# Chunk-major mLSTM rows in DRAM, masks of the first attention head on two engines, and a first modulation made in two halves

## The chip, the cores and the metric

One core of a Trainium2 chip runs the whole layer. The metric is the device time of one execution in microseconds. PE is TensorE, DVE is VectorE, ACT is ScalarE, POOL is GpSimd and SP is SyncE; SP does no arithmetic here, its queue issues most of the DMAs.

## The reference, cut to what matters

One layer over 2048 latent tokens of 1024 features and 256 context tokens. An adaLN modulation is computed from a conditioning vector, the tokens are normalised and modulated and projected; eight heads of neighbourhood attention and four heads of a bidirectional mLSTM read the projection; an output projection and a mixture of experts follow.

```python
ada = silu(c) @ w_ada[l] + b_ada[l]             # latent tokens; ada_c from c_ctx for the context
sh1, sc1, g1, sh2, sc2, g2 = jnp.split(ada, 6, axis=-1)
z  = _modulate(_layer_norm(x), sh1, sc1) @ w_in[l]      # xn * (1 + scale) + shift
zc = _modulate(_layer_norm(ctx), csh1, csc1) @ w_in[l]
...
# neighbourhood attention, per head and grid row: window scores + relative bias, and context scores
s = concatenate([s_win + bias, s_ctx]); p = softmax(s)
...
# mLSTM: q, k = rope(silu(conv5(z)));  then per direction, per chunk of 128 tokens:
dlog = where(causal, b[:, None] - b[None, :] + i[None, :], -inf)
s    = (q_c @ k_c.T) * exp(dlog - m_t)
num  = s @ v_c + inter * (q_c @ C)
C    = decay * C + (wgt * k_c).T @ v_c
...
mix = concatenate([na, ml]) @ w_out[l];  x_mid = LN(alpha * x + g1 * mix)
out = LN(alpha * x_mid + g2 * moe(modulate(LN(x_mid), sh2, sc2)))
```

## The kernel before, in words

The kernel is written with a tile framework: tiles come from pools with a number of buffers, and a planner at compile time puts the instructions of each engine in an order, by the order of the program and by the times it reckons with. An instruction that is wrapped in `in_order` keeps its place in the program. Each engine, and the SP queue, then runs its own list strictly in order.

**Input projection (0 to about 793 us).** The tokens are worked in two halves of 1024, each in two groups of 512; the context is a third group of the first half. Products are made in three passes of split float32 (a high part and a rest of both factors): `mm_T` (L246 to L248) gives columns by tokens and `mm_N` (L255 to L257) tokens by columns; both read the modulated and transposed tokens `xhi`, `xlo` and the weights `whi`, `wlo`. `load_w` (L227) loads a weight block of 128 x 512 into one of three `wraw` buffers, casts it on ACT (L234) and makes its rest on DVE (L235). `build_group` (L159) transposes normalised tokens on PE (L170) and applies the modulation `modT` on ACT (L177, L179), with the rest on DVE (L182). `modT` comes from `first_modulation` (L185): the vectors c and c_ctx are loaded into `cc` with single elements scattered over partitions (L188, L189), passed through SiLU, and multiplied with the first 2048 columns of w_ada, 32 blocks of 128 x 512 float32 (256 KB each, loads at L207, products at L210, four column groups of PE for four blocks). One copy (L214), four transposes (L218) and two copies (L219, L220) then give all of `modT`, and only after it can `build_group` make its first piece. In the loop at L517 the first group's pieces are built pair of k by pair of k and multiplied as they come.

**mLSTM columns.** For each half and each of q and k, four heads: a product, a convolution of five taps on ACT and DVE (L631 to L638), a rotary turn with a partition shuffle through four DMAs (L645), `t1 = acc * cos` (L647, one buffer `t1`), `sw * sin` on POOL (L648), a sum (L649), and a store of 128 partitions x 1022 or 1026 float32 to `mqk_d`, laid out [partition, q or k, head, token] (L650).

**mLSTM stage (about 793 to 972 us).** 32 steps alternate between the two directions; each handles one chunk of 128 tokens for four heads. `fetch_step` (L100) runs three steps ahead into three buffers: `qk` (512 KB, runs of 128 float32 out of `mqk_d`, L104), `bcs` (256 KB, L106), `va` (256 KB, runs of 128 float32 into padded rows, L108). In a step DVE makes the exponents (four instructions of L796), the product with the scores (L816), three small operations (L836 to L838), the state's update (four of L784) and, from the 17th step on, a sum (L851); POOL makes `vw` (L802) and `qw` (L808). All of them are `in_order`. Between the steps `head(0)` (L703), a generator that is advanced once a step from step 2 on, loads the first attention head: q and k rows, nine bias tiles (i = 0 to 8), value rows; and adds a mask to each bias tile on POOL (`masked`, L719 to L721): tiles 0 to 4 from step 10 on and the others in steps 15 to 18. The masks come in three DMAs in steps 6, 10 and 14 (L862).

**Neighbourhood attention (about 972 to 1300 us).** 8 heads x 16 blocks, `scores(n)` (L940): products on PE, bias and maximum on DVE (L960, one input in PSUM and one in SBUF), exponential on ACT, transposes on PE. Head 0's blocks 0 to 3 use bias tiles 0 to 2, blocks 4 to 11 tiles 3 to 5, blocks 12 to 15 tiles 6 to 8. Then the output projection, the router and the expert loop follow in order.

The functions that the change touches:

Of the kernel before, what the change touches and what calls it, by code (L numbers as in the profile page):

```python
# [11 lines left out]
F32 = mybir.dt.float32  # L12
# [10 lines left out]
P = 128  # L23
# [12 lines left out]
def tile_layer(ctx, tc, A, out):  # L36
# [20 lines left out]
    mqk_d = dram.tile([P, 2, 4, NT], F32, name="mqk_d")  # L57
# [42 lines left out]
    def fetch_step(n):  # L100
# [3 lines left out]
        in_order(nc.sync.dma_start(qk[:], mqk_d[:, :, :, c * P : (c + 1) * P]))  # L104
# [7 lines left out]
    with ExitStack() as es, ExitStack() as zes:  # L112
# [72 lines left out]
        def first_modulation():  # L185

            cc = stp.tile([P, 2, KC], F32, name="cc", bufs=1)
            nc.sync.dma_start(cc[:, 0, :], A["c"].rearrange("o (k p) -> p (o k)", p=P))  # L188
            nc.sync.dma_start(cc[:, 1, :], A["c_ctx"].rearrange("(k p) -> p k", p=P))  # L189
            nc.gpsimd.memset(cs[:], 0.0)  # L190
            for i in range(2):
                nc.scalar.activation(cs[:, :, i], cc[:, i, :], AF.Silu)
            pa = pt.tile([P, 2, 2, P], F32, name="ptx")
            pa = pa[:].rearrange("p a b t -> p (a b t)")
            for i in range(2):
                bada = zp.tile([1, 1024], F32, name=("cosq", "sinq")[i])
                nc.sync.dma_start(bada[:], A["b_ada"][:, i * 1024 : (i + 1) * 1024])
                for j in range(2):
                    c0 = 64 * i + 32 * j
                    nc.tensor.matmul(  # L200
                        pa[c0 : c0 + 32, :], ones1[:], bada[:, j * 512 : (j + 1) * 512], start=True, stop=False, tile_position=(0, c0)
                    )
            for k in range(KC):
                wts = []
                for j in range(4):
                    wt = xg.tile([P, 512], F32, name=f"x{('hi', 'lo')[j // 2]}_{j % 2}_{k}")
                    nc.sync.dma_start(wt[:], A["w_ada"][0, k * P : (k + 1) * P, j * 512 : (j + 1) * 512])  # L207
                    wts.append(wt)
                for j in range(4):
                    nc.tensor.matmul(  # L210
                        pa[32 * j : 32 * j + 32, :], cs[:, k, :], wts[j][:], start=False, stop=k == KC - 1, tile_position=(0, 32 * j)
                    )
# [4 lines left out]
            for q in range(4):  # L217
                nc.tensor.transpose(pm[:, q, :], rows[:, q * P : (q + 1) * P], ident[:])  # L218
# [2001 lines left out]
```

## Time and profile before

| what | value |
|---|---|
| median of 3 runs (2724.01 to 2726.02) | 2725.88 us |
| the profiled execution: its own time | 2719.89 us |
| its span | 2717.9 us |
| PE busy in the span | 2481.7 us (91%) |
| DVE busy in the span | 1268.3 us (47%) |
| DMA, mean | 231 GB/s |

The span is the time from the first to the last recorded instruction; the own time of that execution is 1.99 us longer. PE's busy time says that something is in the array, not that the array is at its peak. The slices of the page divide the span into 40 parts of 67.95 us each; a digit is the busy share in tenths:

```profile
PE   8999999999997899998999679979999999999890
DVE  5547224257236976665578952222222233222226
DMA  8634762334449979994654689999689886998936
```

The first slice holds the first modulation, slices 12 to 14 (counted from 0) the mLSTM stage, the slices after that the attention.

### The profile page before, as it was taken

The numbers are of one execution on the slowest core, as the hardware profiler recorded it, in microseconds if no ns is written. First come the engines' busy times: TensorE is split into PE (matmuls) and PEld (weight loads), VectorE is DVE, ScalarE is ACT, GpSimd is POOL, SyncE is SP. The second block draws the span as 40 slices with busy tenths as digits, with TensorE's granted clock in tenths as the row PEclk, the third lists the DMA queues.
The fourth block names the chain that finished last, engine by engine and source line by source line (L and its number), as shares of the span: only waits on it lengthen the run. The fifth ranks groups of instructions, "written<-read, shape, count | busy, mean of one in ns | idle before, by whom it ended". The sixth has DMA issues, their size and how long they took to land. (4 is left out here: it accounts for less than half of the span.)

```text
span 2717.9 us, 51820 instructions
## 1 busy us (share of the span) xinstructions
PE 2481.7 (91%) x17292; PEld 1568.7 (58%) x17292; DVE 1268.3 (47%) x2882; ACT 804.9 (30%) x1707; POOL 759.1 (28%) x886
## 2 busy tenths in 40 slices
PE   8999999999997899998999679979999999999890
PEld 4778667877887778876787533323333333333330
DVE  5547224257236976665578952222222233222226
ACT  4423105243134666655565310000000000000005
POOL 1212211002034535456434422211222122221124
PEclk9999999999999999999999779989999999999995
DMA  8634762334449979994654689999689886998936
GB/s 268 178 102 134 248 219 94 140 97 158 112 137 260 265 197 214 202 212 141 183 152 151 213 308 349 366 394 340 220 281 335 312 299 223 331 328 318 381 102 263
DMA packets 286891, 626.97 MB, mean 231 GB/s; under 512 B 79448, under 2 KB 142924, under 8 KB 262444
## 3 DMA queue, kind: packets, MB, share of 16 engines
q1 hardware_dynamic: 254716, 564.87, 62.6%
q0 software_dynamic: 31696, 60.09, 9.6%
q8 instruction: 70, 1.15, 0.2%
q10 hardware_dynamic: 352, 0.39, 0.1%
q14 instruction: 57, 0.47, 0.1%
HBM read 947.01 MB, written 97.42 MB: 384 GB/s over the span
## 5 line engine op out<-in xcount | busy, mean ns | idle before, releaser
L2048 POOL DMA_INDIRECT acc_d<-y,ids x112 | 174.6, 1559 | 739.9 <-DMA acc_d<-y,ids 277.7
L2011 DVE TENSOR_TENSOR sg<-sg,ph 128x128 f32<-128x128 f32 x112 | 39.8, 355 | 442.7 <-ACT sg L2010 427.2
L2010 ACT ACTIVATE sg<-ph 128x128 f32<-128x128 f32 x112 | 37.1, 331 | 690.5 <-PE ph L2005 522.3
L2005 PE MATMUL ph<-qkk,xT 128*64 128x512 f32 (+1 forms) x1344 | 233.9, 525 | 2.8 <-DMA qkk<-in_w_dram 2.8
L2005 PE MATMUL ph<-mask,xT 128*64 128x512 f32 x896 | 210.8, 613 | 21.5 <-DMA mask<-in_w_dram 21.5
L246 PE MATMUL ps<-xhi,whi 128*128 128x512 f32 (+1 forms) x576 | 221.7, 386 | 1.7 <-DVE ev L509 1.6
L247 PE MATMUL ps<-xlo,whi 128*128 128x512 f32 (+1 forms) x576 | 220.4, 383 | 0.2 <-DVE xlo L182 0.2
L248 PE MATMUL ps<-xhi,wlo 128*128 128x512 f32 (+1 forms) x576 | 220.2, 382 | 0.0
L2037 PE MATMUL py<-mo,gT 128*64 128x512 f32 x672 | 166.2, 631 | 24.4 <-DMA mask<-in_w_dram 12.3
L255 PE MATMUL ps<-whi,xhi 128*128 128x512 f32 x416 | 166.1, 401 | 1.5 <-ACT whi L234 1.5
L256 PE MATMUL ps<-wlo,xhi 128*128 128x512 f32 x416 | 164.3, 396 | 3.2 <-DVE wlo L235 3.2
L257 PE MATMUL ps<-whi,xlo 128*128 128x512 f32 x416 | 164.8, 397 | 0.0
L960 DVE CUSTOM_DVE_ANT_0 sb<-ps,bias 128x640 f32<-128x640 f32 (+1 forms) x128 | 113.9, 891 | 102.9 <-PE ps L957 82.7
L2005 PEld LDWEIGHTS ph<-mask,xT 128*64 128x64 f32 x896 | 61.8, 140 | 144.5 <-issue 142.8
L2005 PEld LDWEIGHTS ph<-qkk,xT 128*64 128x64 f32 (+1 forms) x1344 | 74.9, 128 | 114.4 <-issue 98.5
L2021 DVE COPY gT<-pg 128x128 f32<-128x128 f32 x112 | 40.2, 359 | 210.6 <-PE pg L2019 205.7
L1972 DVE TENSOR_SCALAR xT<-pxt,mod 128x96 f32<-128x96 f32 x456 | 135.0, 369 | 2.5 <-PE pxt L1965 2.5
L246 PEld LDWEIGHTS ps<-xhi,whi 128*128 128x128 f32 x576 | 108.3, 188 | 28.7 <-issue 3.2
L2045 DVE SCALAR_TENSOR_TENSOR y<-py,wgt,g2r 128x256 f32<-128x256 f32 x112 | 68.7, 613 | 119.9 <-PE py L2037 119.9
L2010 ACT ACT_TABLE_LOAD x28 | 35.9, 1283 | 299.5 <-PE ph L2005 299.5
L247 PEld LDWEIGHTS ps<-xlo,whi 128*128 128x128 f32 x576 | 108.3, 188 | 23.0 <-DVE xlo L182 0.9
L248 PEld LDWEIGHTS ps<-xhi,wlo 128*128 128x128 f32 x576 | 108.3, 188 | 23.0 <-DVE wlo L235 0.3
(549 smaller groups left out, 5087.2 us busy)
## 6 DMA issues: line engine op xcount, KB each, us to landing
w<-in_w_dram SPq DMA_DIRECT2D x203, 1024.0 KB, 7.5
mask<-in_w_dram SPq DMA_DIRECT2D x114, 1024.0 KB, 8.7
qkk<-in_w_dram SPq DMA_DIRECT2D x114, 1024.0 KB
mo<-in_w_dram SPq DMA_DIRECT2D x171, 512.0 KB, 4.1
bias<-in_w_dram SPq DMA_DIRECT2D x58, 1024.0 KB
xo<-in_w_dram SPq DMA_DIRECT2D x115, 512.0 KB, 8.2
bias<-in_w_dram SPq DMA_DIRECT2D x58, 512.0 KB
qkk<-in_w_dram SPq DMA_DIRECT2D x58, 512.0 KB
```

What stands on the lines that cost most here:

```text
L246: nc.tensor.matmul(ps, wh_, xhi[g, k][:], start=k == 0, stop=False)
L247: nc.tensor.matmul(ps, wh_, xlo[g, k][:], start=False, stop=False)
L248: nc.tensor.matmul(ps, wl_, xhi[g, k][:], start=False, stop=k == KC - 1)
L255: nc.tensor.matmul(ps, xh, his[k], start=k == 0, stop=False)
L256: nc.tensor.matmul(ps, xh, los[k], start=False, stop=False)
L257: nc.tensor.matmul(ps, xl, his[k], start=False, stop=k == KC - 1)
L960: in_order(nc.vector.tensor_tensor_reduce(out=sb[:, 0:L], in0=ps[:, off:768], in1=bt[:, 0:L], scale=-0.125, scalar=3.0e38, op0=OP.add, op1 ...
L1972: i = nc.vector.tensor_scalar(xT[u][:, k], pxt[:, k, 0:96], mod2[:, 1, k : k + 1], mod2[:, 0, k : k + 1], OP.mult, OP.add)
L2005: in_order(nc.tensor.matmul(ph[j * n : (j + 1) * n], xT[u][:, k, t0 : t0 + n], w13[k][:, :, j * NH : (j + 1) * NH], start=k == 0, stop=k = ...
L2010: nc.scalar.activation(sg[:], ph[:, 0, :], AF.Silu)
L2037: in_order(nc.tensor.matmul(py[j * n : (j + 1) * n, :], gT[:, b_, j_ * n : (j_ + 1) * n], w2t[c][:, j * NY : (j + 1) * NY], start=c == 0, ...
L2048: sc = nc.gpsimd.indirect_dma_start(out=acc_d[:].rearrange("t (g n) -> (t g) n", g=G), out_offset=bass.IndirectOffsetOnAxis(ap=ids[u][:, l ...
```

## The change

It has three parts.

1. `mqk_d` is laid out [chunk, partition, q or k, head, token in the chunk]. A fetch of a step then reads one contiguous run of 1024 float32 for each partition (512 KB in all as before). The stores go through `mqk_store`, which splits the tokens at chunk borders: the first half's store becomes a DMA of seven whole chunks and one of 126 tokens, the second half's one of 2 tokens (8 bytes for each partition) and one of eight whole chunks, all in runs of 128 float32 at most. The context's stores and the two loads in `context_state` follow the layout.
2. The masks of the first head: tiles 0 to 2 are masked on DVE instead of POOL, at the same places; tiles 3 to 8 stay on POOL, but are masked in the first six blocks of the attention, one ahead of each `scores(n)`.
3. `first_modulation` becomes a generator. `cc` is loaded with contiguous runs (16 partitions x 128), passed through SiLU and transposed on PE. The blocks of w_ada are loaded and multiplied in two parts of 16 blocks; part 0 gives `modT` for k = 0 to 3 and part 1 for k = 4 to 7. The loads of x come after `cc` and `b_ada` in the program. Two weight blocks are loaded and cast (`w_first`) ahead of part 0's copies; the products of k = 0 to 3 of the first group come ahead of part 1; part 1's loads and products stand after the loads of all eight weight blocks, and the second group's x loads after part 1.

```diff
@@ -54,7 +54,23 @@
     nv_d = dram.tile([NT, 512], F32, name="nv_d")
-    mqk_d = dram.tile([P, 2, 4, NT], F32, name="mqk_d")
+    mqk_d = dram.tile([NT // P, P, 2, 4, P], F32, name="mqk_d")
+    def mqk_store(qk, h, o0, o1, src):
+        while o0 < o1:
+            c, a = o0 // P, o0 % P
+            n = (o1 - o0) // P if a == 0 else 0
+            if n:
+                nc.sync.dma_start(
+                    mqk_d[c : c + n, :, qk, h, :].rearrange("c p t -> p c t"), src[:, 0 : n * P].rearrange("p (c t) -> p c t", t=P)
+                )
+                m = n * P
+            else:
+                m = min(P - a, o1 - o0)
+                nc.sync.dma_start(mqk_d[c, :, qk, h, a : a + m], src[:, 0:m])
+            o0, src = o0 + m, src[:, m:]
     mv_d = dram.tile([NT, 512], F32, name="mv_d")
@@ -101,7 +117,7 @@
         qk = ml["l"].tile([P, 2, 4, P], F32, name="qk")
-        in_order(nc.sync.dma_start(qk[:], mqk_d[:, :, :, c * P : (c + 1) * P]))
+        in_order(nc.sync.dma_start(qk[:], mqk_d[c]))
         bcs = ml["l"].tile([P, 4, P], F32, name="bcs")
@@ -184,40 +200,51 @@
-            cc = stp.tile([P, 2, KC], F32, name="cc", bufs=1)
-            nc.sync.dma_start(cc[:, 0, :], A["c"].rearrange("o (k p) -> p (o k)", p=P))
-            nc.sync.dma_start(cc[:, 1, :], A["c_ctx"].rearrange("(k p) -> p k", p=P))
             nc.gpsimd.memset(cs[:], 0.0)
+            cc = stp.tile([2 * KC, P], F32, name="cc", bufs=1)
+            nc.sync.dma_start(cc[0:KC, :], A["c"].rearrange("o (k p) -> (o k) p", p=P))
+            nc.sync.dma_start(cc[KC : 2 * KC, :], A["c_ctx"].rearrange("(k p) -> k p", p=P))
+            bada = []
             for i in range(2):
...
+                bada.append(zp.tile([1, 1024], F32, name=("cosq", "sinq")[i]))
+                nc.sync.dma_start(bada[i][:], A["b_ada"][:, i * 1024 : (i + 1) * 1024])
+            yield
+            nc.scalar.activation(cc[:], cc[:], AF.Silu)
+            pc = pt.tile([P, 2, 2, P], F32, name="ptx")
+            pc = pc[:].rearrange("p a b t -> p (a b t)")[:, 0 : 2 * KC]
+            nc.tensor.transpose(pc, cc[:], ident[0 : 2 * KC, 0 : 2 * KC])
+            nc.vector.tensor_copy(cs[:, :, 0:2], pc.rearrange("p (i k) -> p k i", i=2))
+            for part in range(2):
+                pa = pt.tile([P, 2, 2, P], F32, name="ptx")
+                pa = pa[:].rearrange("p a b t -> p (a b t)")
                 wts = []
...
+                for k in range(KC):
+                    for i in range(2):
+                        wt = xg.tile([P, 512], F32, name=f"x{('hi', 'lo')[i]}_{part}_{k}")
+                        c0 = i * 1024 + part * 512
+                        nc.sync.dma_start(wt[:], A["w_ada"][0, k * P : (k + 1) * P, c0 : c0 + 512])
+                        wts.append(wt)
+                for k in range(-1, KC):
+                    for i in range(2):
+                        if k < 0:
+                            l, r = ones1[:], bada[i][:, part * 512 : (part + 1) * 512]
+                        else:
+                            l, r = cs[:, k, :], wts[2 * k + i][:]
+                        nc.tensor.matmul(
+                            pa[32 * i : 32 * i + 32, :], l, r, start=k < 0, stop=k == KC - 1, tile_position=(0, 32 * i)
+                        )
+                if part == 0:
+                    yield
+                rows = tp.tile([P, 512], F32, name="t")
+                nc.vector.tensor_copy(rows[0:64], pa[0:64])
+                pm = pt.tile([P, 2, 2, P], F32, name="ptx")
+                pm = pm[:].rearrange("p a b t -> p (a b) t")
+                for q in range(4):
+                    nc.tensor.transpose(pm[:, q, 0:64], rows[0:64, q * P : (q + 1) * P], ident[0:64, 0:64])
+                c0 = 32 * part
+                nc.vector.tensor_copy(modT[:, :, c0 : c0 + 32], pm[:, :, 0:32])
+                nc.vector.tensor_scalar(modT[:, :, 64 + c0 : 96 + c0], pm[:, :, 32:64], 1.0, None, OP.add)
+                yield
@@ -375,7 +402,7 @@
                 c = 16 + i
-                nc.sync.dma_start(kt[:, i], mqk_d[:, 1, :, c * P : (c + 1) * P])
+                nc.sync.dma_start(kt[:, i], mqk_d[c, :, 1])
                 nc.gpsimd.memset(va[i][:, :, 128:129], 1.0)
@@ -480,8 +507,12 @@
+        first_mod = first_modulation()
+        next(first_mod)
         xq = [normalised(rows_of_x(0, 0))]
-        first_modulation()
+        next(first_mod)
+        w_first = load_w(weights(0), (0, 1))
+        next(first_mod)
         rows_of, builds = {0: xq[0]}, {}
@@ -511,24 +542,41 @@
-            w = weights(0)
-            if half:
-                load_w(w)
+            w = load_w(weights(0)) if half else w_first
             for q, (g, n, t0) in enumerate(groups[0:2]):
...
+                def products(k2):
+                    for c in range(4):
+                        mm_T(pss[c][:], g, w, c * P, (k2, k2 + 1))
+                if half == 0 and q == 0:
+                    built(g, 1)
+                    load_w(w, (2, 3))
+                    built(g, 2)
+                    pss.extend(pz.tile([P, 512], F32, name="ps") for _ in range(4))
+                    products(0)
+                    load_w(w, (4, 5))
+                    products(2)
+                    load_w(w, (6, 7))
+                    next(first_mod)
+                    coming = rows_of_x(0, 1)
+                    built(g, 3)
+                    built(g, 4)
+                    products(4)
+                    rows_of[1] = normalised(coming, True)
+                    built(groups[1][0], 1)
+                    products(6)
+                else:
+                    for k2 in range(0, KC + 2, 2):
+                        built(g, k2 // 2 + 1)
+                        if half or k2 == KC:
+                            built(groups[1][0], k2 // 2 + 1 if half else 1)
+                        if k2 == 2:
+                            pss.extend(pz.tile([P, 512], F32, name="ps") for _ in range(4))
+                        if k2:
+                            products(k2 - 2)
                 for c in range(4):
@@ -638,7 +686,7 @@
                             nc.vector.tensor_scalar(acc[:, 0:m], acc[:, 0:m], P ** -0.5, None, OP.mult)
-                            nc.sync.dma_start(mqk_d[:, 1, h, SEQ:NT], acc[:, 0:m])
+                            mqk_store(1, h, SEQ, NT, acc[:, 0:m])
                             continue
@@ -647,7 +695,7 @@
                         nc.vector.tensor_tensor(t1[:, 0:m], t1[:, 0:m], sw[:, 0:m], OP.add)
-                        nc.sync.dma_start(mqk_d[:, qk, h, o0:o1], t1[:, 0:m])
+                        mqk_store(qk, h, o0, o1, t1[:, 0:m])
@@ -696,6 +744,7 @@
     heads = {}
+    first_masks = []
@@ -718,7 +767,12 @@
             w = (12, 16, 12)[i // 3] * 32
-            in_order(nc.gpsimd.tensor_tensor(bias[i][:, 0:w], bias[i][:, 0:w], mask[:, i, 0:w], OP.add))
+            e = nc.vector if h == 0 and i < 3 else nc.gpsimd
+            add = lambda: in_order(e.tensor_tensor(bias[i][:, 0:w], bias[i][:, 0:w], mask[:, i, 0:w], OP.add))
+            if h == 0 and i >= 3:
+                first_masks.append(add)
+            else:
+                add()
@@ -1052,6 +1106,8 @@
                 coming_head = head(n // 16 + 1)
+            if n < len(first_masks):
+                first_masks[n]()
             if n < 128:
```

## Rows read from the trace of the kernel before

**Rows 1.** Windows: length, busy per engine (instructions), granted clock, DMA share, GB/s; the long stage.
```profile
41.00:800.00 759.00, 749.44 (x3430) 579.62 (x3431) 339.74 (x523) 244.38 (x398) 123.26 (x165) 1.00 0.47 147
```

**Rows 2.** Windows of 4 us in the first 40 us.
```profile
8.00:12.00 4.00, 2.04 (x9) 0.36 (x10) 3.40 (x6) 1.60 (x3) 1.59 (x4) 1.00 0.77 173
...
20.00:24.00 4.00, 4.00 (x13) 0.82 (x12) 0.00 (x0) 0.00 (x0) 0.00 (x0) 1.00 1.05 388
```

**Rows 3.** Timeline of the start: start us, us, engine, line, operation, tiles.
```profile
4.79 3.16 SPq L197 DMA_DIRECT2D cosq<-in_b_ada_dram  x1
...
8.28 1.57 SPq L207 DMA_DIRECT2D xhi<-in_w_ada_dram  x2
...
29.77 1.68 SPq L231 DMA_DIRECT2D wraw<-in_w_in_dram  x3
...
35.62 0.69 DVE L214 COPY t<-ptx 128x512 f32<-128x512 f32 x1 [20.05 <-PE ptx L210]
...
38.78 4.19 SPq L231 DMA_DIRECT2D wraw<-in_w_in_dram  x3
...
40.96 1.17 PE L246 MATMUL ps<-xhi,whi 128*128 128x512 f32 x4
```

**Rows 4.** Waits of the SP queue, 0 to 90 us: total us, times, longest.
```profile
SPq L231 <- DVE wlo L235: 18.2, 8, 4.4
```

**Rows 5.** Timeline of DVE in the mLSTM stage: five of the 32 products of L816.
```profile
804.03 0.68 DVE L816 TENSOR_TENSOR ex<-ex,ps 128x512 f32<-128x512 f32 x1
...
822.95 0.68 DVE L816 TENSOR_TENSOR ex<-ex,ps 128x512 f32<-128x512 f32 x1
...
856.76 0.68 DVE L816 TENSOR_TENSOR ex<-ex,ps 128x512 f32<-128x512 f32 x1
...
909.71 0.68 DVE L816 TENSOR_TENSOR ex<-ex,ps 128x512 f32<-128x512 f32 x1
...
969.36 0.68 DVE L816 TENSOR_TENSOR ex<-ex,ps 128x512 f32<-128x512 f32 x1
```

**Rows 6.** Waits, 780 to 1000 us.
```profile
DVE ex L796 <- DMA bcs<-bc_d: 21.7, 5, 7.5
```

**Rows 7.** Windows: three stretches of the mLSTM stage.
```profile
857.00:910.00 53.00, 39.17 (x330) 37.45 (x331) 51.54 (x110) 30.28 (x94) 32.65 (x33) 1.00 1.10 266
820.00:857.00 37.00, 25.38 (x174) 24.47 (x173) 15.76 (x60) 15.49 (x47) 12.45 (x14) 0.86 1.03 250
920.00:960.00 40.00, 36.57 (x292) 33.43 (x290) 39.45 (x105) 26.58 (x82) 18.91 (x17) 1.00 0.89 271
```

**Rows 8.** Timelines of DVE (L796) and POOL (L721, L808) in the mLSTM stage.
```profile
838.40 0.35 DVE L796 SCALAR_TENSOR_TENSOR ex<-bcs,cols,cmask 128x128 f32<-128x128 f32 x1 [7.52 <-DMA bcs<-bc_d]
...
903.95 1.27 POOL L808 TENSOR_TENSOR qw<-qk,it 128x512 f32<-128x512 f32 x1 [2.37 <-issue]
...
903.99 1.38 DVE L796 SCALAR_TENSOR_TENSOR ex<-bcs,cols,cmask 128x128 f32<-128x128 f32 x1
...
905.18 1.05 POOL L721 TENSOR_TENSOR bias<-bias,mask 128x384 f32<-128x384 f32 x1
```

**Rows 9.** Lines by form, 0 to 500 us: busy us, mean ns | idle before.
```profile
L182 DVE TENSOR_TENSOR xlo<-t,xhi 128x256 fp32r<-128x256 f32 x72 | 28.6, 423 | 5.4 <-ACT xhi L179 4.2
```

**Rows 10.** Timelines of POOL and DVE where the mLSTM stage ends.
```profile
969.26 1.31 POOL L808 TENSOR_TENSOR qw<-qk,it 128x512 f32<-128x512 f32 x1 [2.58 <-ACT it L807]
...
974.32 0.69 DVE L851 TENSOR_TENSOR h<-h,hs 128x512 f32<-128x512 f32 x1 [0.67 <-ACT h L847]
...
981.60 0.96 DVE L960 CUSTOM_DVE_ANT_0 sb<-ps,bias 128x768 f32<-128x768 f32 x1 [0.37 <-PE ps L957]
```

**Rows 11.** Timelines of SP and DVE, and a window, in the second half's convolutions.
```profile
633.25 0.36 SPq L650 DMA_DIRECT2D mqk_d<-t  x1
...
640.57 1.23 DVE L647 TENSOR_TENSOR t<-acc,cosq 128x1026 f32<-128x1026 f32 x1 [2.24 <-DMA mqk_d<-t]
...
652.00:654.00 2.00, 0.59 (x3) 0.16 (x1) 2.00 (x1) 1.92 (x3) 2.00 (x1) 1.00 0.00 0
```

More of the change, by code (lines that the diff above doesn't have):

```diff
@@ L191, in first_modulation @@
+            bada = []
             for i in range(2):
[L192 to L202, printed above, removed]
@@ L203, in first_modulation @@
-            for k in range(KC):
-                wts = []
[L205 to L212, printed above, removed]
@@ L213, in first_modulation @@
-            rows = tp.tile([P, 512], F32, name="t")
-            nc.vector.tensor_copy(rows[:], pa)
-            pm = pt.tile([P, 2, 2, P], F32, name="ptx")
-            pm = pm[:].rearrange("p a b t -> p (a b) t")
-            for q in range(4):
-                nc.tensor.transpose(pm[:, q, :], rows[:, q * P : (q + 1) * P], ident[:])
-            nc.vector.tensor_copy(modT[:, :, 0:64], pm[:, :, 0:64])
-            nc.vector.tensor_scalar(modT[:, :, 64:P], pm[:, :, 64:], 1.0, None, OP.add)
+                bada.append(zp.tile([1, 1024], F32, name=("cosq", "sinq")[i]))
@@ L511, in evacuated @@
                 nc.sync.dma_start((qlo_d, klo_d)[qk][c][:, t0 : t0 + W], lo[:, 0:W].bitcast(F32))
-            w = weights(0)
-            if half:
-                load_w(w)
+            w = load_w(weights(0)) if half else w_first
             for q, (g, n, t0) in enumerate(groups[0:2]):
                 pss = []
-                for k2 in range(0, KC + 2, 2):
-                    if half == 0 and q == 0 and k2 < KC:
-                        load_w(w, (k2, k2 + 1))
-                    built(g, k2 // 2 + 1)
-                    if half or k2 == KC:
-                        built(groups[1][0], k2 // 2 + 1 if half else 1)
-                    if k2 == 2:
-                        pss = [pz.tile([P, 512], F32, name="ps") for _ in range(4)]
-                    if k2:
-                        for c in range(4):
-                            mm_T(pss[c][:], g, w, c * P, (k2 - 2, k2 - 1))
-                    if half == 0 and q == 0 and k2 == 2:
-                        rows_of[1] = normalised(rows_of_x(0, 1), True)
+                def products(k2):
[27 more added lines that the diff above has]
+                            products(k2 - 2)
                 for c in range(4):
```

## The prediction

> **What bounds the kernel now.** I read the page's slices first, then windows, then timelines and waits. The slices say that PE is busy nearly everywhere and that the first slice and the mLSTM stage are not alike: so each part of the change is priced in its own stage. From 41 to 800 us PE is busy 749.44 of 759 us [rows 1]: nothing that makes DMA, DVE or ACT lighter there can gain more than those 9.6 us, and a delay of what feeds PE costs. Before 41 us the DMA engines bound the time: at 20 to 24 us they move 388 GB/s at a share of 1.05 [rows 2], and PE's first product of the projection starts at 40.96 us [rows 3]. From 804.03 to 969.36 us the mLSTM steps run in three ways, read from the starts of L816 [rows 5]: 4 steps from 822.95 to 856.76 take 8.45 us each, 9 steps to 909.71 take 5.88 us each, 12 steps to 969.36 take 4.97 us each. The first of these wait for DMA (DVE's exponents wait 21.7 us for `bcs`, five times [rows 6], at a DMA share of 1.03 [rows 7]); in the second DVE is busy 51.54 of 53 us [rows 7], and POOL's masks are in it; the third is the bare pace. Behind the mLSTM stage all follows in order, so I carry every microsecond to the end.
>
> **The first modulation.** Before, 4.2 MB of w_ada (16 blocks of 256 KB) stand in the queue that are no longer needed for the first product. At 388 GB/s [rows 2] that is 10.8 us. SP also spends 3.16 us on one issue behind the scattered `cc` loads and issues the first block of w_ada at 8.28 us [rows 3]. With contiguous runs it can start near 4.5 us, but the 2.1 MB of x in front occupy the engines to about 7: I take 1.6 us. The first product then starts 12.4 us earlier, at 28.5. PE has 48 products to do on k = 0 to 3 (four column blocks, four k, three passes). At 749.44 / 3430 = 0.22 us each [rows 1] they and their transposes take 11 us, to 39.5. Part 1 then has to be there. Behind part 0 (landed at about 20.5) stand 2.1 MB of weights and 4.2 MB of part 1, 16.2 us at 388 GB/s: 36.7. From there to a product takes 6.5 us (copy at 35.62 to product at 40.96 is 5.3 [rows 3], and the last products of the modulation some 1.2): 43.2. PE stands 3.7 us, net gain 8.7. That holds if the planner puts part 1's loads ahead of weight loads that wait for one of three `wraw` buffers. If they stay behind, then what counts is that eight weight loads took from 29.77 to 42.97 before [rows 3], held by DVE's rests (18.2 us of waits, eight times [rows 4]). Taken with 11 us, part 1 starts at 31, lands at 42.5 and feeds a product at 49: PE stands 9.5 us, net gain 2.9. Between the two I take 6, with ends of +3 (a loss, see the third rival) and -12.4. Casting two weights ahead of the copies costs nothing that was not done before: in the rows the copy at 35.62 stands beside the same casts. DVE and ACT get this work earlier.
>
> **The stores.** Each of the 16 stores becomes two DMAs, in 512 byte runs instead of about 4 KB. The extra 16 issues cost SP 0.36 us each [rows 11], 6 us of a queue that mostly waits. What counts is the one `t1` buffer: the next L647 waits until the store has landed. The store issued at 633.25 held it until 640.57, and later in that stretch PE is busy only 0.59 of 2 us [rows 11]: there a late store is paid in full. Bounds per store are 0 and another 7 us (the row's landing in series). I take 0.5 us for the shorter runs in the second half's few heads where DVE waits, 1 us in all: the two DMAs are not dependent on each other and overlap.
>
> The page "DMA: Bandwidth & Descriptors" of the Trainium skill (Specifications) says that writes under 512 bytes are done by read-modify-write, which speaks against the eight stores of 8-byte runs. No row of before has such a store; if it held, it would raise the chance of the fourth rival, not the sum.
>
> **The fetches.** In 920 to 960 us a step moves 271 GB/s x 4.97 us = 1.35 MB in 0.89 x 4.97 = 4.42 us of the DMA engines' time [rows 7]. At the rate of 2 KB runs, 388 / 1.05 = 370 GB/s per unit of share [rows 2], it would be 3.65. The surplus of 0.77 us belongs to the loads in 512 byte runs, `qk` (512 KB) and `va` (256 KB): two thirds, 0.52 us, is `qk`'s. Bounds: 0 (if the surplus is `va`'s padded rows) and 0.77. Ten fetches are issued up to the end of the DMA-bound stretch: 10 x 0.52 = 5.2 us less in front of the last of them, so 5.2 of the stretch's loss (33.81 - 4 x 4.97 = 13.9 us) goes. What is late next is still the queue of the head's own loads. Bounds: 0 and 13.9.
>
> By the Trainium skill's page "DMA: Bandwidth & Descriptors", "Why small descriptors are slow", each packet carries about 3 extra cycles at 32 bytes a cycle. An estimate from it: 8 x 19 against 131 cycles, 14% of `qk`'s 1.94 us, 0.27 us for a fetch and 2.7 in place of 5.2. The row's surplus is twice that; I go by the row.
>
> **The masks.** Nine steps lose 5.88 - 4.97 = 0.91 us each [rows 5], 8.2 us. The row shows how: an exponent of DVE with two SBUF inputs takes 0.35 us alone and 1.38 while POOL's two-input L808 runs [rows 8], and L721 adds another 1.05 us of that. Three masks come back on DVE: 128x256 takes 0.42 [rows 9], 128x512 0.69 [rows 10], so 0.55 for 128x384; each can stand behind L808's 1.27. Between 0.55 and 1.8 I take 0.6, since L816 then runs beside the POOL work that it waited for: 1.8 us. They also wait for bias and mask loads that were issued four steps earlier; behind a waiting mask stand L816 and all of DVE's step. With steps of 4.97 us the DMA engines need 1.10 x 53 - 9 x 0.52 = 53.6 us [rows 7] in 46.5 us of steps, more than the share of 1.10 that this stretch showed: at 1.10 it takes 48.7, so 2 us are given back. The six masks that move into the attention take 6.9 us of POOL (three of 384 columns at 1.05, three of 512 at L808's 1.27 [rows 8]), from about 970.6 on, when L808 has ended [rows 10]. Block 4 reads the first of them at 981.60 [rows 10]: they are in time. But the last sums of the mLSTM (L851, both inputs in SBUF, until 975.01 [rows 10]) now run beside them and can each be held by one mask: 0 to 4 us, I take 2. What else POOL has there, the next head's memsets, waits a few us, and those loads are needed a head later. Net of the masks: 8.2 - 1.8 - 2 - 2 = 2.4 us.
>
> **The sum.** 6 + 5.2 + 2.4 - 1 = 12.6, say 13 us. The profiled execution took 2719.89 us (span 2717.9), so it would become 2707. The median of the runs shown is 5.99 us above it; carried there, 2725.88 - 13 = 2713.
>
> **The rivals.**
> First, more comes (chance 0.17): the queue gets short enough that the DMA wait goes wholly (13.9), part 1 is loaded ahead (8.7), no share limit binds (masks 4.4): 26 us with the stores off, 2700. For it: waits for DMA grow with the queue, so a small relief can end them. Against it: the head's loads (about 3.3 MB) are unchanged.
> Second, the masks give nothing (0.15): with POOL freed, DMA becomes the bound in 857 to 910 us. For it: the share of 1.10 there. Then 6 + 5.2 - 2 - 1 = 8 us, 2718.
> Third, the start gives nothing (0.13): part 1 stays behind eight weight loads, and the casts behind `build_group` on DVE and ACT. A product on k = 4 at 55 us would mean 15.5 us of standing PE against 12.4 won: +3. With 7 from the rest, 2722, which can't be told from no change.
> Fourth, slower (0.10): the two stores of a head land one after the other. `t1` comes free up to 7 us later in the seven heads of the second half that follow a store; as DVE's convolutions already stall PE there [rows 11], I price half, 25 us, against 14 of gain: 2737. It decides from 2 us per head. Against it: the DMAs go to different places from the same source, and DMA is idle much of that stretch (a share of 0.47 on average [rows 1]).
>
> **How the numbers follow.** My forecast has 0.45, 2713, its own range 2705 to 2720. A measurement of this kernel can tell about 0.2%, 5.5 us, from no change. Faster: the forecast, the first and the second rival, 0.76 after their edges; same 0.14 (the third and an edge); slower 0.10. The range of 2697 to 2724 leaves out the far end of the first rival (0.06) and the fourth with an edge (0.13).
>
> **What would show it.** First product (L246) near 28 us instead of 40.96, then a hole in PE near 40 to 43; a hole to 49 shows the queue order. DVE's waits for `bcs` at about 15 instead of 21.7 us. Steps near 5 us from about 850 us on, no L721 on POOL before 970, three on DVE. L851 longer than 0.69 at the stage's end. L647's waits for the stores not above 1 us more. The prediction is wrong if the stage from L815's first to last step is not 5 to 10 us shorter, if PE stands more than 12 us between 28 and 60 us, or if PE's hole near 652 us grows by more than 3 us.

## The result, and the profile after

The kernel after takes 2708.17 us (median of 4 runs, 2702.98 to 2710.40) against 2725.86 us before (4 runs, 2724.01 to 2726.02): ratio 0.9934, 95% interval 0.9917 to 0.9951, so 13 to 23 us less. The prediction was 2713 us, 13 us less. The direction and the size of the whole hold; the sizes of its four terms do not, and their errors cancelled; that the whole came so near is luck in that sense. The profiled execution of after took 2710.4 us itself (span 2708.6), the slowest of its four, and that of before took less than its timed runs. So the two traces differ by 9.5 us only, and stages are compared over all profiled kernels, in the table of the next section.

The slices of the page of after, in the same 40 parts, are nearly those of before: what changed lies inside the first slice and slices 12 to 14, and finer views are needed.

```profile
PE   8999999999997899988999579979999999999890
DVE  6446324357235876655578943312222223322226
DMA  8634762435459989984654689999589886998936
```

The start, from the timeline of PE: start, us, line and operation (L273 to L275 are the products of L246 to L248, L233 those of the modulation, L243 its transposes).

```profile
27.40 0.73 PE L273 MATMUL ps<-xhi,whi 128*128 128x512 f32 x2 [0.18 <-DVE xhi L197]
...
38.48 0.40 PE L275 MATMUL ps<-xhi,wlo 128*128 128x512 f32 x1
38.80 0.61 PE L233 MATMUL ptx<-cosq,ones 1*32 1x512 f32 x1
...
46.24 0.59 PE L233 MATMUL ptx<-xhi,cs 128*32 128x512 f32 x1
...
47.65 0.46 PE L243 MATMUL ptx<-ident,t 64*128 64x64 f32 x4 [0.81 <-DVE t L239]
...
51.20 0.73 PE L273 MATMUL ps<-xhi,whi 128*128 128x512 f32 x2 [0.23 <-DVE xhi L197]
```

The first product starts at 27.40 us, 13.56 earlier than in [rows 3]. From 38.88 to 51.20 us no product of the projection runs. PE hardly stands there (busy 10.62 of the 12.40 us from 38.80 on): the 18 products of part 1, two records each, hold it from 38.80 to 46.8, and transposes follow. The product at 51.20 is the 49th of the projection. Before, the 49th started at 53.75:

```profile
53.75 0.48 PE L246 MATMUL ps<-xhi,whi 128*128 128x512 f32 x1
```

So of the 13.56 us, 2.55 are left when the interruption is over.

The mLSTM stage, from the windows of all engines: us, then busy time (instructions) of PE, PEld, DVE, ACT and POOL, the granted clock, DMA share, GB/s. They answer to [rows 7].

```profile
804.00:820.00 16.00, 12.46 (x104) 12.10 (x103) 8.05 (x30) 7.47 (x24) 5.67 (x6) 0.95 1.06 210
820.00:857.00 37.00, 27.74 (x199) 26.88 (x199) 18.88 (x70) 18.59 (x57) 14.37 (x17) 0.84 1.05 269
848.00:892.00 44.00, 38.76 (x324) 37.02 (x324) 31.16 (x111) 29.43 (x90) 22.51 (x23) 1.00 1.05 278
915.00:950.00 35.00, 32.36 (x260) 29.79 (x259) 34.21 (x93) 23.29 (x71) 16.89 (x15) 1.00 0.80 261
```

DMA is as full as before from 804 to 857, and in the stretch of the masks (848 to 892) DVE, which was busy 51.54 of 53 us, is busy 31.16 of 44 at a share of 1.05. The waits of the stage (total, times, longest) say for what it waits; the second line answers to [rows 6].

```profile
POOL vw L856 <- DMA va<-mv_d: 46.3, 17, 8.5
DVE ex L850 <- DMA bcs<-bc_d: 43.5, 19, 7.5
...
PE ps L869 <- DMA qk<-mqk_d: 18.5, 9, 4.9
```

Two of the three masks on DVE, and L870 (L816 before) behind each:

```profile
847.83 0.55 DVE L771 TENSOR_TENSOR bias<-bias,mask 128x384 f32<-128x384 f32 x1
848.30 0.68 DVE L870 TENSOR_TENSOR ex<-ex,ps 128x512 f32<-128x512 f32 x1
...
852.00 0.55 DVE L771 TENSOR_TENSOR bias<-bias,mask 128x384 f32<-128x384 f32 x1
852.47 0.68 DVE L870 TENSOR_TENSOR ex<-ex,ps 128x512 f32<-128x512 f32 x1
```

A step with a mask in it takes 852.47 - 848.30 = 4.17 us, where the steps of [rows 5] in this stretch took 5.88; the first one without (to 860.35) takes 3.70, so a mask costs 0.47 by this one subtraction. At the end of the stage POOL's masks stand beside DVE's last two sums (L905, L851 before), which took 0.69 in [rows 10]:

```profile
958.01 1.16 DVE L905 TENSOR_TENSOR h<-h,hs 128x512 f32<-128x512 f32 x1
959.36 1.21 DVE L905 TENSOR_TENSOR h<-h,hs 128x512 f32<-128x512 f32 x1 [0.19 <-ACT h L901]
```

```profile
954.46 5.57 POOL L771 TENSOR_TENSOR bias<-bias,mask 128x512 f32<-128x512 f32 x4
960.72 0.77 POOL L785 MEMSET bias<- 128x384 f32 x2 [0.69 <-DVE h L905]
961.45 1.01 POOL L771 TENSOR_TENSOR bias<-bias,mask 128x384 f32<-128x384 f32 x1
```

### The profile page after: what moved, and what is told of

Read it like the earlier page. It is cut to its first block, busy times and chain, and to the rows that moved or that the text cites. A ratio compares the mean times of both kernels' runs of the same rounds, so it can differ in the third digit from the quotient of the medians.

```text
span 2708.6 us, 51845 instructions
## 1 busy us (share of the span) xinstructions
PE 2478.5 (92%) x17297; PEld 1569.1 (58%) x17297; DVE 1238.7 (46%) x2889; ACT 806.3 (30%) x1706; POOL 759.1 (28%) x883
## 5 line engine op out<-in xcount | busy, mean ns | idle before, releaser
L273 PE MATMUL ps<-xhi,whi 128*128 128x512 f32 (+1 forms) x576 | 221.9, 386 | 1.0 <-DVE ev L540 0.6
L275 PE MATMUL ps<-xhi,wlo 128*128 128x512 f32 (+1 forms) x576 | 220.2, 382 | 0.3 <-DVE wlo L262 0.3
L273 PEld LDWEIGHTS ps<-xhi,whi 128*128 128x128 f32 x576 | 108.1, 188 | 28.4 <-issue 3.2
L1022 ACT ACTIVATE sb<-sb,nm 128x640 f32<-128x640 f32 (+1 forms) x128 | 113.2, 885 | 35.7 <-DVE nm L1014 31.7
L275 PEld LDWEIGHTS ps<-xhi,wlo 128*128 128x128 f32 x576 | 108.2, 188 | 23.8 <-DVE wlo L262 0.8
```

Source lines behind the costliest of these rows:

```text
L273: nc.tensor.matmul(ps, wh_, xhi[g, k][:], start=k == 0, stop=False)
L275: nc.tensor.matmul(ps, wl_, xhi[g, k][:], start=False, stop=k == KC - 1)
L1022: in_order(nc.scalar.activation(sb[:, 0:L], sb[:, 0:L], AF.Exp, bias=nm[:], scale=-1.0, accum_out=rss[n // 8][:, n % 8 : n % 8 + 1]))
```

## The experiments

Single executions of one kernel differ by up to 24 us here (before: 2714 to 2738 us over these runs; the expert loop alone, the same code, takes 1055.6 to 1063.6 us in the profiles). So the total is read from ratios, and each term from its stage: the time at which the first rotated columns are stored (start), PE's busy time from 560 to 690 us (hole), and the times between the starts of L816 (steps, counted from 0). The start, PE's busy time and the steps are read from one profile of each kernel.

| kernel | ratio to before [95%] | first store, us | PE busy of 130 us | steps 2-10 | 10-19 | 19-31 | 0-31 |
|---|---|---|---|---|---|---|---|
| before | 1 | 194.6 | 126.34 | 52.7 | 53.0 | 59.6 | 173.2 |
| after | 0.9934 [0.9917, 0.9951] | 190.4 | 129.41 | 53.5 | 44.3 | 60.6 | 166.4 |
| e1 modulation alone | 0.9988 [0.9975, 1.0001] | 191.1 | 126.52 | 56.7 | 52.9 | 59.7 | 177.2 |
| e2 rows in DRAM alone | 0.9971 [0.9954, 0.9988] | 195.1 | 128.69 | 52.0 | 53.0 | 59.7 | 172.6 |
| e3 masks alone | 0.9981 [0.9965, 0.9997] | 195.7 | 125.85 | 51.1 | 47.2 | 60.9 | 167.1 |
| e4 after, old rows | 0.9966 [0.9950, 0.9983] | 192.1 | 127.46 | 54.1 | 45.8 | 60.7 | 168.4 |
| e5 wide loads | 1.1321 [1.1301, 1.1341] | 191.2 | 129.61 | 97.4 | 44.4 | 59.8 | 209.4 |
| e6 split stores | 0.9991 [0.9977, 1.0006] | 194.0 | 126.42 | 52.4 | 53.4 | 59.6 | 173.3 |
| e7 both parts in front | 0.9950 [0.9932, 0.9968] | 193.9 | 129.72 | 51.4 | 44.2 | 60.6 | 164.0 |
| e8 as e5, spread | 1.1309 [1.1286, 1.1333] | 189.8 | 129.76 | 95.6 | 41.3 | 60.7 | 205.5 |
| e9 rows in pairs | 0.9836 [0.9807, 0.9865] | 188.8 | 129.69 | 41.6 | 47.5 | 60.0 | 157.0 |
| e10 pairs, spread | 0.9815 [0.9786, 0.9844] | 189.7 | 129.93 | 39.5 | 45.4 | 61.1 | 154.0 |
| e11 spread | 0.9910 [0.9883, 0.9936] | 191.0 | 129.71 | 46.4 | 48.0 | 59.9 | 162.1 |
| e12 as e10, old rows | 0.9853 [0.9828, 0.9877] | 190.3 | 126.29 | 38.3 | 45.4 | 62.2 | 153.8 |

**Each part alone (e1 to e4).** Edits: the kernel before with the hunks of `first_modulation` and of the loops that call it (e1), of `mqk_d` (e2), of `masked` (e3); after without those of `mqk_d` (e4). Theory A is the reading of the two traces alone.

> The kernel before with only the first modulation in halves and two weights cast ahead. The prediction has 6 us less (8.7 with the second half's loads ahead of waiting weight loads, 2.9 with them behind). The trace after has them ahead, and the first product of the mLSTM's scores 9.3 us earlier: theory A says 9 us less (2717), all of it already at the first step of the mLSTM, steps unchanged behind it. Rival: part of the 9.3 came from elsewhere in the projection, then 3 to 6 us.

> The kernel before with only the chunk-by-chunk rows and their stores. The prediction has 5.2 us less from the fetches and 1 more from the stores: 4 us less (2722), with DVE's waits for bcs down from 21.7 to about 15 us. Theory A, from the trace after, says that the 4 KB pieces take as long as eight of 512 bytes while other loads compete: 0 to 1 us less, four steps from 822 to 857 us as long as before (8.4 us each), waits for bcs at 20 us or more.

> The kernel before with only the first head's masks moved. The prediction has 2.4 us less, with the share limit of the DMA engines giving back 2 of 8.2. Theory A says that the nine steps from 857 to 910 us become 8 us shorter and that at most 1 comes back behind them: 7 us less (2719). Rival: without the chunk-by-chunk rows the DMA engines become the bound there, 2 to 3 us less.

> The kernel after with the rows in DRAM and their stores as before: modulation and masks changed only. If the layout is worth nothing (theory A): the same time as the kernel after, within 2 us. If it is worth the prediction's 4 us: 4 us more than the kernel after. If the shorter steps need it (the DMA engines bound with POOL free): 6 us or more above it, in the steps from 850 us on.

e1: theory A's 9 us is wrong. By time e1 is 3 us faster (0 to 7). The first store is 3.5 us earlier, the first step of the mLSTM 5.6 (790.59 against 796.17), and steps 2 to 10 are 4.0 us longer in this run. Over all kernels the first store stands at 194.0 to 195.7 (mean 194.9) in the four without the start's change, at 188.8 to 192.1 (mean 190.5) in the nine that have it as it is: 4.4 us. The prediction's 6 is nearer than 9.

e2: faster by 8 us (3 to 13), where theory A had 0 to 1 and the prediction 4; yet the steps it was meant for give only 0.7 us of 52.7, and the waits for `bcs` stay at 21.4 us. Part of the gain is elsewhere: PE is busy 128.69 of 130 us in place of 126.34. The same holds for every kernel with the new rows (128.69 to 129.93, mean 129.6, eight kernels) against every one without (125.85 to 127.46, mean 126.5, six): 3.1 us, most of it from a hole near 655 us. PE's waits in 560 to 690 us are, before:

```profile
PE ps L256 <- DVE wlo L235: 2.2, 1, 2.2
PE ps L255 <- ACT whi L234: 1.5, 1, 1.5
```

and after:

```profile
PE ps L275 <- DVE wlo L262: 0.3, 1, 0.3
PE ps L283 <- DVE wlo L262: 0.2, 1, 0.2
```

DVE's timeline shows why. Before, three rests of weights (L235) stand in one block behind the convolution (L635, L647):

```profile
645.67 3.93 DVE L635 SCALAR_TENSOR_TENSOR acc<-z,cw,acc 128x1026 f32<-128x1026 f32 x3
649.51 1.22 DVE L647 TENSOR_TENSOR t<-acc,cosq 128x1026 f32<-128x1026 f32 x1
650.65 1.28 DVE L635 SCALAR_TENSOR_TENSOR acc<-z,cw,acc 128x1026 f32<-128x1026 f32 x1
651.85 4.06 DVE L235 TENSOR_TENSOR wlo<-wraw,whi 128x512 fp32r<-128x512 f32 x3
```

In e2 they stand one by one between the convolution's instructions (L651 is L635, L251 is L235):

```profile
647.00 1.28 DVE L651 SCALAR_TENSOR_TENSOR acc<-z,cw,acc 128x1026 f32<-128x1026 f32 x1
648.19 0.68 DVE L251 TENSOR_TENSOR wlo<-wraw,whi 128x512 fp32r<-128x512 f32 x1
648.80 1.28 DVE L651 SCALAR_TENSOR_TENSOR acc<-z,cw,acc 128x1026 f32<-128x1026 f32 x1
649.99 0.68 DVE L251 TENSOR_TENSOR wlo<-wraw,whi 128x512 fp32r<-128x512 f32 x1
```

The lines of these products are not in the change. With other stores the planner put DVE's list in another order. The block's first rest also took 2.86 us in place of 0.69. Of the 112 rests of before three take more than 0.75 us (1.39, 2.86 and 2.91), each beside an instruction of POOL with two inputs, as the 1.38 us of [rows 8] did; three others that overlap one take 0.68 or 0.69.

```profile
651.85 2.86 DVE L235 TENSOR_TENSOR wlo<-wraw,whi 128x512 fp32r<-128x512 f32 x1
```

```profile
651.13 3.03 POOL L648 TENSOR_TENSOR sw<-sw,sinq 128x1026 f32<-128x1026 f32 x1 [6.64 <-DMA sw<-acc]
```

The surplus of 2.2 us is as long as PE's wait for L235. The block stands in all six kernels with the old rows (4.05 to 4.08 us for the three), in none of after, e2 and e9. That the order is what fills the hole is read from these rows; no run changed the order alone.

e3 and e4: e3 is 5 us faster by time (1 to 10), where theory A had 7 and the rival 2 to 3. In the steps the masks take 5.8 (e3 against before), 7.1 (e4 against e1) and 8.7 us (after against e2) off steps 10 to 19 and add 0.9 to 1.3 to steps 19 to 31. e4 stands 0.0032 above after, with overlapping intervals: by time alone the rows' 4 us cannot be told from 8. Three pairs differ in the rows and their stores alone: e2 and before, after and e4, e10 and e12 below. Their ratios are 0.0029, 0.0032 and 0.0038 apart, 8 to 10 us each. The stages show 3.1 of that in the hole and 0.7 or less in the steps; where the rest lies was not found.

**The stores (e6).** Edit, on the kernel before:

```diff
-                        nc.sync.dma_start(mqk_d[:, qk, h, o0:o1], t1[:, 0:m])
+                        for a, b in ((0, 512), (512, m)):
+                            nc.sync.dma_start(mqk_d[:, qk, h, o0 + a : o0 + b], t1[:, a:b])
```

> The kernel before with each store of a head's columns split into two DMAs (columns 0 to 511 and the rest), rows in DRAM as before. The prediction charged 0.5 us for each split store where DVE waits. Theory C, from the trace after: smaller pieces land sooner (2.8 us in place of 4.4), so the single t1 buffer comes free earlier; here landing near 3 us, DVE's waits for the store below 5 us in all and PE busy some 2 us more of 560 to 690 us. Rival: it is the order of the chunk-by-chunk rows that lands sooner, and a split alone leaves 4.4 us.

The hole stays (126.42), with the block of three rests in place. Theory C is wrong in both halves. Its 4.4 and 2.8 us came from landings that the profile gives for a few DMAs on `mqk_d`, other stores and loads among them: in before for one of these 16 stores. The traces keep the semaphore updates of all DMAs. From the first issue of a store to the last update of its DMAs passed, over 16 stores, in the median 3.5 us before (2.6 to 7.3), 3.7 in e6 (2.7 to 7.4) and 4.0 in after (3.6 to 6.4): split stores land no sooner, and those in 512 byte runs, with their second DMA, 0.5 later. DVE's waits for them (total, times, longest) are, before, in e6 and in after:

```profile
DVE t L647 <- DMA mqk_d<-t: 5.7, 6, 2.2
```

```profile
DVE t L647 <- DMA mqk_d<-t: 5.2, 4, 2.0
```

```profile
DVE t L695 <- DMA mqk_d<-t: 4.7, 5, 1.9
```

The other traces have 4.9 to 9.5 us, with either layout, so a difference of 1 says nothing.

**The start (e7).** Edit, on the kernel after: a second `next(first_mod)` ahead of the first group's loop, and the one between `load_w(w, (6, 7))` and `coming = ...` taken out.

> The kernel after with the second half of the modulation finished ahead of the first products (loads, products and transposes of both halves in front; the contiguous loads of c and the casts ahead stay). If the halves are what wins at the start (prediction): the first product near 39 us again, PE without a hole at 44 to 52, and the first step of the mLSTM 3 us later than in the kernel after. Rival: the hole eats what the halves win, the first product is later but the first store of mqk_d at the same time within 1 us.

First product at 39.91 us, first store at 193.9: 3.4 us behind the mean with halves, 1.0 ahead of the mean without the change. By the first store the halves are nearly all of the start's gain; contiguous `cc` and earlier casts are worth about 1 us, less than the spread of the four kernels without the change (1.7). But the lead does not last: the first step of the mLSTM starts 2.2 us later than in after (789.13 against 786.91), the last one at the same time (953.15 against 953.27), and the intervals of the two ratios overlap. That the halves make the whole kernel faster is not shown by this run.

**What fills the DMA engines (e5, e9).** By the DMA records of the trace of after, the pieces of `qkk` (9 KB each, a head's k rows over 64 partitions) take 0.69 us each, that is 13 GB/s for an engine; 2 KB pieces go at 0.084 us (median), 24 GB/s. e5 replaces the six loads of a head by three over 128 partitions, with the two sources, or two copies, as the outer step:

```diff
-    qhi_d = [dram.tile([P, SEQ], F32, name=f"qhi{i}") for i in range(4)]
-    qlo_d = [dram.tile([P, SEQ], F32, name=f"qlo{i}") for i in range(4)]
+    q_d = [dram.tile([2, P, SEQ], F32, name=f"qhl{i}") for i in range(4)]
+    qhi_d, qlo_d = [t[0] for t in q_d], [t[1] for t in q_d]
-        load(q[0:64, :].bitcast(F32), qhi_d[pair][f0 : f0 + 64, :])
...
+        load(q.bitcast(F32), q_d[pair][:, f0 : f0 + 64, :])
-            for p0 in (0, 64):
-                load(dst[p0 : p0 + 64, :].bitcast(F32), src[pair][f0 : f0 + 64, :])
+            row = src[pair][f0 : f0 + 64, :]
+            load(dst.bitcast(F32), bass.AP(tensor=row.tensor, offset=row.offset, ap=[[0, 2], *row.ap]))
             yield
+        yield
```

> The kernel after, with q, and both copies of k, of each attention head loaded by one DMA over all 128 partitions each (three DMAs in place of six over 64 partitions). Theory B: the stretch of the mLSTM steps that waits for DMA is set by these loads, which run at half the rate that the 2 KB runs reach (8 and 9 KB pieces into 64 partitions); spread over all partitions, 3.4 MB take 9 us in place of 17, the steps 2 to 10 take 45 us in place of 53.5, and the kernel 8 us less than the one after. Rival: the bytes alone bound the stretch, and it stays at 52 us or more.

A miss: 360 us above before, where some 8 below after were expected. The attention takes 630 us in place of 299, and three steps of the mLSTM take 21 to 28 us each. Windows of e5, columns as above:

```profile
820.00:850.00 30.00, 6.37 (x36) 6.20 (x36) 3.15 (x12) 3.29 (x10) 2.75 (x3) 0.61 0.22 81
850.00:880.00 30.00, 6.75 (x37) 6.62 (x37) 3.15 (x12) 3.29 (x10) 2.67 (x3) 0.61 0.43 131
```

The DMA engines are 0.22 and 0.43 busy while everything waits for them. By the records, the 256 pieces of k ran from 826 to 878 us at 0.38 us each: 98 us of work in 52, two engines at a time. e9 changes the order, so that 64 is outside and 2 inside (rows 2p and 2p + 1 belong to feature p, in q and k alike). It also takes out e5's second `yield`, so what `head(0)` does behind these loads comes one step sooner than in e5 and after:

```diff
-    q_d = [dram.tile([2, P, SEQ], F32, name=f"qhl{i}") for i in range(4)]
-    qhi_d, qlo_d = [t[0] for t in q_d], [t[1] for t in q_d]
+    q_d = [dram.tile([P, 2, SEQ], F32, name=f"qhl{i}") for i in range(4)]
+    qhi_d, qlo_d = [t[:, 0] for t in q_d], [t[:, 1] for t in q_d]
-        load(q.bitcast(F32), q_d[pair][:, f0 : f0 + 64, :])
+        load(q.bitcast(F32), q_d[pair][f0 : f0 + 64].rearrange("p a t -> (p a) t"))
-            load(dst.bitcast(F32), bass.AP(tensor=row.tensor, offset=row.offset, ap=[[0, 2], *row.ap]))
+            load(dst.bitcast(F32), bass.AP(tensor=row.tensor, offset=row.offset, ap=[row.ap[0], [0, 2], row.ap[1]]))
             yield
-        yield
```

> The kernel after, with q and both copies of k of a head loaded by one DMA over 128 partitions each, but with the rows in pairs (row 2p and 2p+1 of a tile are the high and the low part, or the two copies, of feature p), so that the outer step of a DMA counts 64 and not 2 as in the wide loads that made the heads' loads slow. Theory D: a DMA whose outer step counts 2 is worked by two of the 16 DMA engines only; with 64 outside all 16 work, its 9 KB pieces take 0.4 us as in the wide run and not 0.7, steps 2 to 10 take 45 us in place of 53.5 and the kernel is 8 us below the one after. Rival: the pieces take 0.7 us because all 16 engines work at once and the bytes bound the stretch; then it stays at 52 us or more and the time is that of the kernel after within 2 us. A second rival: any DMA over three levels of addresses is slow; then some 360 us more again.

Theory D holds: 9 KB pieces at 0.37 us, steps 2 to 10 in 41.6 us, and windows of e9

```profile
792.00:834.00 42.00, 35.76 (x300) 33.90 (x300) 35.80 (x101) 26.91 (x83) 20.21 (x22) 1.00 1.03 332
834.00:881.00 47.00, 40.61 (x324) 39.47 (x322) 31.52 (x110) 29.25 (x90) 22.59 (x22) 0.93 0.99 264
881.00:941.00 60.00, 54.40 (x433) 49.86 (x432) 56.44 (x157) 39.53 (x121) 28.16 (x24) 1.00 0.81 256
```

of which the first moves 332 GB/s at the share at which after moved 210 to 278. The gain is larger than expected (ratio 0.9836, 45 us below before and some 27 below after), since the attention of the other heads gains too: 299.3 to 284.1 us, DVE's waits for POOL's bias there 21.0 to 4.6 us.

The Trainium skill, "SBUF — State Buffer", "Door 1: The DMA port swizzle", says that DMA bandwidth follows the number of ports that the partitions of a transfer reach and that 64 partitions in a row do not reach all of them. The halved time of the same 9 KB piece in e9 agrees. Its page "DMA: Bandwidth & Descriptors", "Rules for kernel authors", says that an outermost step of a count below 16, such as a leading broadcast of c copies, keeps the whole DMA on at most c engines; e5's two engines agree.

**Spread (e8, e10, e11).** Edit, on e5 (without its second `yield`), e9 and after in turn:

```diff
-            if n in (6, 10, 14):
-                i0 = (n - 6) // 4 * 3
+            if n in (10, 18, 26):
+                i0 = (n - 10) // 8 * 3
-            if n >= 2:
+            if n >= 2 and (n % 2 == 0 or n > 26):
                 next(first_head, None)
```

> The kernel after with the wide loads and with the first head's loads and masks spread over steps 2 to 30 of the mLSTM in place of 2 to 18 (masks' loads at steps 10, 18, 26). Theory B: no stretch waits for DMA any more, steps near 4.6 us throughout, the stage from the first to the last step 145 to 152 us in place of 166, the kernel 14 us or more below the one after. Rival: the total of bytes bounds the stage, what is taken from the first steps is added to the last ones, and nothing more than the wide loads' gain is left.

> The rows in pairs, and the first head's loads and masks spread over steps 2 to 30 in place of 2 to 18 (masks' loads at steps 10, 18, 26). Theory B: steps near 4.6 us throughout, 145 to 152 us from first to last step in place of 166, 14 us or more below the kernel after. Rival: the bytes of the whole stage bound it; then what the first steps win is lost in the last ones and the stage stays within 4 us of the pairs alone.

> The kernel after with only the spreading (steps 2 to 30, the loads over 64 partitions as they were). If the stretch of waits came from the loads being bunched: the stage 8 us shorter or more. If the bytes bound the whole stage: the same length within 3 us, with the waits for DMA spread over it.

e8 fell with e5 (ratio 1.1309) and says nothing on spreading. e10 is the fastest of all kernels (2678.53 us), but its stage is 154.0 us, 3.0 below e9, and the intervals of e9 and e10 overlap. So the rival's number came; its reason, the bytes, did not. DVE's waits for `bcs`, in e9 and in e10:

```profile
DVE ex L848 <- DMA bcs<-bc_d: 23.1, 13, 4.2
```

```profile
DVE ex L848 <- DMA bcs<-bc_d: 3.1, 2, 2.7
```

What stays is not DMA: in the middle window of e9, taken in e10, DVE is busy 46.38 of 47 us at a DMA share of 0.81.

```profile
834.00:881.00 47.00, 41.00 (x342) 38.89 (x342) 46.38 (x114) 31.21 (x96) 24.38 (x25) 1.00 0.81 242
```

e11's stage is 4.3 us shorter than that of after, between the two expectations.

**The fetches (e12).** Edit: e10 without the hunks of `mqk_d`.

> The kernel with rows in pairs and the loads spread, but with the mLSTM rows in DRAM and their stores as before the change. The prediction's term for the fetches (0.52 us each where DMA bounds) would make the steps of the mLSTM 5 to 14 us longer than with the chunk-by-chunk rows (154.0 us from first to last step). Theory A: a fetch in 512 byte pieces costs the engines no more than in 4 KB pieces while others load, so the steps stay within 2 us of 154, and only the hole of PE near 655 us comes back (PE busy 126 in place of 129.9 of 130 us from 560 to 690): some 4 us in all.

153.8 us against 154.0: fetching in 4 KB runs is worth nothing in the steps, also where hardly a wait for a load is left. The hole is back (126.29). By time e12 stands 10 us above e10, of which the hole is 3.6; the intervals overlap.

## Why the prediction was right, step by step

- **Start: 6 taken, 4.4 measured.** The first product (28.5 taken, 27.40) was right; the interruption was not (PE was to stand 3.7 us and go on at 43.2; it went on at 51.20, 12.3 behind 38.88). The planner did put part 1's loads ahead, the hoisted case, and the data were not what was late. I charged 1.2 us for "the last products of the modulation", as if the others ran beside the loads. All 18 stood behind the 48 products and took 8.0 us of PE, two column groups at a time. That 6 came near is luck: it was the mean of two cases, and the one that came was priced at 8.7. The other one's 2.9 rests on a misread row: by 42.97 the SP timeline of before has seven weight loads, and the eighth at 50.03.
- **Fetches: 5.2 taken, 0.7 or less measured for steps 2 to 10** (0.7 in e2, 0.6 from e4 to after, and 1.2 the other way from e12 to e10). This is the term that failed. The surplus of 0.77 us was a division of shares, which does not say which load costs what. The stretch was set by the first head's own loads over half of the partitions; I had them ("the head's loads are unchanged") and did not price them. The estimate of 2.7 from the Trainium skill's cost of a small packet ("DMA: Bandwidth & Descriptors", "Why small descriptors are slow") was too high as well.
- **Masks: 2.4 taken, about 6 measured** (5.8 to 8.7 off steps 10 to 19, 0.9 to 1.3 back in steps 19 to 31). 0.55 us for each mask on DVE was right, and a step lost 0.47 by it. DVE did come to wait for DMA, as the second rival had it (1.05 in 848 to 892, waits for `bcs` 21.7 to 43.5 us), but the nine steps took 44.3 us, where the term with its limit and its masks meant 53 - 8.2 + 1.8 + 2 = 48.6. Nine steps at the "bare pace" of 4.97 are 44.7: that pace, read from the last twelve steps, was no floor for these, of which one with a mask took 4.17 and one without 3.70. L851 is longer by 0.47 and 0.52, 1 us in place of 2.
- **Stores: 1 lost taken, 3.1 won measured.** The stores did land later, by the 0.5 us taken (3.5 to 4.0 in the median), but DVE's waits for them did not grow (5.7 and 4.7), so nothing was lost; the fourth rival's serial landing did not happen. (The Trainium skill's rule on writes under 512 bytes, "DMA: Bandwidth & Descriptors", Specifications, was named there. No run tests it by itself; the eight DMAs of 8 byte runs landed in 1.4 to 4.9 us by their semaphores, each ahead of the large one issued behind it.) The hole at [rows 11] was put down to a late store; by the rows it belonged to weights' rests late in DVE's list, one of them slow beside POOL.

The sum by terms as measured is 4.4 + 0.7 + 6 + 3.1 = 14 us, inside the interval of 13 to 23; start and fetches were taken too large by 6 to 7 us together, masks and stores too small by 8. The starts of L816 give another sum: the first step stands at 797.0 us in the mean of before, e3 and e6, and at 786.5 in the six kernels with the whole start and the new rows; with the 6.8 us that the stage is shorter in after, that makes 17. Some 3 us were won between the first store and the first step, outside the hole, and were not traced. What would have shown the prediction wrong did not come: the stage went from 173.2 to 166.4 us, PE was busy 31.04 of 33 us from 27 to 60, the hole near 652 us shrank. The waits for `bcs`, foreseen at 15 us, showed 43.5.

Open: steps 2 to 10 are longer by 4.0 (e1 against before), 3.0 (e4 against e3) and 1.5 us (after against e2) where the start's change is in. That was seen and not explained; counted in, the sum by terms is 10 to 13, at or below the interval's lower end, so the terms do not cover the whole gain.

## What to carry to other kernels

A stretch bound by DMA is priced by the load that is slow in it, not by the one that the change touches: compare GB/s at a full share with the best stretch of the same kernel (210 to 278 here against 388), and look for loads that write half of the partitions. A low rate alone does not name them (e9 still moves 264 at 0.99 from 834 to 881 us); the time of one piece of a given size does. When data are made to arrive earlier, the work that PE must do on them is a term of its own. And with a planner that orders queues by reckoned times, any edit can open or close a hole hundreds of microseconds away, so a part's gain is looked for in all stages before it is explained by its purpose.

## What the runs showed of the hardware

- Two DMAs of 1152 KB whose outer step counts 2 took 52 us together on two engines at a time; the attention doubled (299 to 630 us). With 64 outside it took 284.
- The same 9 KB piece took 0.69 us when a load wrote 64 partitions and 0.37 when it wrote 128.
- A store of 128 partitions x 4 KB landed 3.5 us (median of 16) behind its first issue as one DMA, 3.7 as two, and 4.0 in 512 byte runs with a small second DMA.
- Of 112 instructions of DVE over 128x512 with two inputs in SBUF (L235 of before), the only three above 0.75 us (1.39, 2.86, 2.91) stood beside an instruction of POOL with two inputs.
- 4 KB and 512 byte pieces of the same fetch: 154.0 and 153.8 us from the first to the last of 32 steps.
